# Modulation steps moved from the second layer's merge into the first layer's second feed-forward network, and another order of the first attention

## The chip, the core and the metric

One core of a Trainium2 chip runs the whole kernel. TensorE (PE in the rows) does the matrix products, VectorE (DVE) and ScalarE (ACT) the elementwise work, GpSimd (POOL) what is left over, and SyncE (SP) issues most loads. The metric is the device time in microseconds. The kernel before took 2209.5 us, the median of three runs from 2206.29 to 2209.86. The profiled execution took 2209.73 us; the span of its trace is 2207.9 us, so 1.8 us lie outside the trace.

## What is computed

Two layers of a trunk over 256 latent tokens and 256 context tokens, model width 1024, all in float32:

```
per layer:
  x += 1/2 * ffn_a(modulated norm(x))            # SwiGLU, width 2816
  u  = modulated norm(x) @ w_in                  # split into q, kv, differential q/k/v, pool, three gates
  x += gate * (sigmoid(g0)*A(u) + sigmoid(g1)*B(u) + sigmoid(g2)*C(u)) @ w_out
  x += 1/2 * ffn_b(modulated norm(x))            # SwiGLU, width 2816
output: final RMS norm of the latent tokens
```

A is latent attention with 8 heads, B differential attention with 8 heads (two softmax maps each), C a pooling over 2, 4, 8 and 16 neighbours. The modulation of a layer is nine vectors of 1024 values (shift, scale and gate for each of the three parts), each the product of a 1024 x 1024 matrix with the conditioning vector of the latent tokens, and with that of the context tokens. In the second layer only the latent tokens go on after the attention's keys are made, so its vectors m = 5 to 8 are needed for one stream only.

## The kernel before, in words

**Weights.** A float32 product is made of three products of split operands (`mm3`, line 292): hi times hi, lo times hi, hi times lo. Every weight comes as a chunk of 128 x 1024 (512 KB). `Weights.split` (line 131) loads it into a raw buffer (line 142, queue of SP), ScalarE casts the upper part `hi` (line 143), and VectorE or GpSimd subtracts it to get `lo` (line 147). GpSimd makes `lo` where `on_pool` is set; in both merges (after their first column) and in all that follows the second attention VectorE does. Four raw buffers (`RAW`) and four pairs hi/lo (`RING`) go round; a chunk is prepared up to three chunks ahead of its product.

**Modulation.** `ada_step` (line 249) is one of 144 steps of eighteen vectors: it loads 128 columns of one modulation matrix, 512 KB, into one of the same four raw buffers (line 259, SP), and VectorE multiplies and sums it with the conditioning vector (line 262, tile `junk`, one instruction per stream). The steps run in one fixed sequence; who calls `ada_step` takes the next one. Callers are the first feed-forward loop at its start, `FFN.step` (line 584) once per hidden block f, `FFN.middle` (line 612) once per output block, and the merge, once for each of its 24 branches (line 1369). When all 144 are done, a call does nothing.

**Stages.** Each layer is: first feed-forward network ("ffa"), attention and pooling ("mixing"), merge, second feed-forward network ("ffb"). A feed-forward network has 22 hidden blocks f of 128; 0 and 1 belong to the boundary, `FFN.middle` runs f = 2 to 13, then the first half of the output product, then f = 14 to 21. In the second layer's ffb each hidden block is half as long on TensorE, since 256 instead of 512 columns go through.

**Order of the attention.** `mixing` (line 1178) issues its instructions in an order written by hand, `SCHEDULE` (line 43): one string per layer, rounds between bars. For each attention unit a round runs the letters; before the round the unit's scores `a1` (tile `sc`) and its softmax `soft` (exponentials `pe` on ScalarE) are issued. `T` transposes the oldest waiting unit's probabilities on TensorE (tile `tr`; ScalarE casts `pth`, VectorE subtracts `ptl`), `V` multiplies them with the values (tile `po`), `N` runs the next piece of a normalisation, `P` and `D` switch `lo` between GpSimd and VectorE, and the other words are projections and their work: `q6` makes a query, `p1` a pooling group (scratch tiles `pp` and `pw`, mostly on GpSimd), `g12` a gate computed early, `k2`, `dk2` keys, and so on. Each engine executes its queue strictly in the order of issue, so the place of a word is its place in all queues.

Of the kernel before, what the change touches and what calls it, by code (L numbers as in the profile page):

```python
# [17 lines left out]
D = 1024  # L18
KD = 8
T = 512  # L20
# [20 lines left out]
WARM = 3  # L41
EARLY = ((68, 108), (271, 307))
SCHEDULE = (
# [138 lines left out]
class Kernel:  # L182
# [372 lines left out]
    class FFN:  # L555
# [28 lines left out]
        def step(self, f):  # L584
            K = self.K
            for up in (False, True):
                it = Kernel.FItem(self, f, up)
                if self.both:
                    it.mm(None)
                else:  # L590
                    it.part(range(KD))
                it.finish()
                self.early(up)
            K.ada_step()

        def early(self, store):
            if self.i == 0:
# [580 lines left out]
    def mixing(self):  # L1178
        nc = self.nc
        l = self.ml  # L1180
        both = len(self.qs) == 2
# [51 lines left out]
        kr, kr_copy = self.kr_item()  # L1233
# [37 lines left out]
        def fetch(dm):  # L1271
            for b in (2, 1, 0):
                if (dm, b) in early:
                    fetched[dm, b] = t = self.pg("sg")
                    nc.sync.dma_start(t[:, c], early.pop((dm, b))[:, c])
# [6 lines left out]
        def settle():  # L1282
            self.run_later()
            done.update(soon)
            soon.clear()

        def step(text):


            for x in text.split():  # L1290
                if x == "N":
                    if cur:
                        cur.pop(0)()
                elif x in "PD":
                    self.on_pool = x == "P"
                elif x == "V":
                    n, pv = pvs.pop(0)
                    if pv:
                        assert need[n][1] in done, (n, need[n])
                        pv()  # L1300
                    if n in last:
                        done.add(last[n])
                elif x == "T":
                    n, u = trs.pop(0)
                    u.tr()
                    pvs.append((n, u.pv))
                else:
                    f, req = fill.pop(x)
                    assert all(y in done for y in req), (x, req)
                    before, self.later = self.later, []  # L1310
                    was = list(soon)
                    soon.clear()
                    f()
                    for y in before:
                        y()
                    done.update(was)
                    soon.append(x)
                    if not self.later:
                        settle()
        rounds = SCHEDULE[l].split("|")  # L1320
        step(rounds.pop(0))
        settle()
        for n, mk in enumerate(units):
            assert all(x in done for x in need[n][0]), (n, need[n])
            u = mk()
            u.a1()
            u.soft()
            if n in heads:
                done.add(f"u{heads[n]}")
            cur.extend(x for x in (u.norm, u.comb) if x)  # L1330
            step(rounds.pop(0))
            while cur:
                cur.pop(0)()
            settle()
            trs.append((n, u))
# [4 lines left out]
        for dm in range(KD):  # L1340
            ms = []
            if dm == 1:
                self.on_pool = False
            for b in (2, 1, 0):
                bias = self.v(V_BG + l * 24 + b * 8 + dm)
                if b == 2:
                    for n in ((0, 1) if dm == 0 else (dm + 1,)):
                        fetch(n)
                g = fetched.pop((dm, b), None)
                if g:  # L1350
                    nc.scalar.activation(g[:, c], g[:, c], AF.Sigmoid, bias=bias)
                else:
                    p = self.ps("gt")
                    self.gemm(p[:, c], self.win(l, C_GATE + b * D + dm * 128), self.u, c)
                    g = self.pg("sg")
                    nc.scalar.activation(g[:, c], p[:, c], AF.Sigmoid, bias=bias)
                if dm == 0:
                    step(rounds.pop(0))
                    settle()
                branch = (self.oml, self.odn, self.opool)[b]  # L1360
                pb_ = self.ps("br")
                self.gemm(pb_[:, c], [(names[b], l, i * 128, ((dm * 128, 128),)) for i in range(4)],
                          [branch[i] for i in range(4)], c)
                if dm == 0:
                    step(rounds.pop(0))
                    settle()
                nc.vector.tensor_tensor(out=g[:, c], in0=g[:, c], in1=pb_[:, c], op=ALU.mult)
                ms.append(g)
                self.ada_step()
                if dm == KD - 1 and b == 2:  # L1370
                    for j in range(KD):
                        self.back("X", self.X, j)
                if dm == KD - 1 and b != 0:
                    for i in ((0, 1, 2) if b == 2 else (3, 4, 5, 6)):
                        h, o = self.pg(f"mh{i}", F32R), self.pg(f"ml{i}", F32R)
                        self.split(merged[i][:, c], h[:, c], o[:, c])
                        merged[i] = (h, o)
            nc.gpsimd.tensor_tensor(out=ms[0][:, c], in0=ms[0][:, c], in1=ms[1][:, c], op=ALU.add)
            nc.vector.tensor_tensor(out=ms[0][:, c], in0=ms[0][:, c], in1=ms[2][:, c], op=ALU.add)
            merged.append(ms[0])  # L1380
# [337 lines left out]
```

## Time and profile before

| stage (window of the trace, us) | length | PE busy | DVE busy | POOL busy |
|---|---|---|---|---|
| start, ffa of layer 1 (0 to 437) | 437 | 404.17 | 285.20 | 177.79 |
| first attention (437 to 770) | 333 | 320.90 | 200.34 | 138.15 |
| first merge, ffb of layer 1 (770 to 1315) | 545 | 537.93 | 326.52 | 243.52 |
| ffa of layer 2 (1315 to 1623) | 308 | 308.00 | 184.27 | 113.76 |
| second attention (1623 to 1886) | 263 | 249.50 | 168.98 | 125.84 |
| second merge (1886 to 1980) | 94 | 84.91 | 70.65 | 16.25 |
| its output product (1980 to 2010) | 30 | 29.54 | 27.85 | 7.79 |
| ffb of layer 2 (2010 to 2133) | 123 | 123.00 | 79.26 | 0.18 |
| end (2133 to 2208) | 75 | 66.86 | 44.89 | 4.43 |
| span | 2207.9 | 2124.8 | 1388.0 | 827.7 |
| **profiled execution's own time** | **2209.73** | | | |

TensorE is busy for 96% of the span. What can be saved without taking products away is the time that it stands, and the time that it runs at half its clock. The mean granted clock of the run is 0.982 of full speed.

### The profile page before, as it was taken

To read this page: it belongs to the slowest core of one execution; us is meant where nothing else is said; L and a number is where in the kernel's file an instruction comes from. 1 tells how busy PE (TensorE), PEld (TensorE's weight loads), DVE (VectorE), ACT (ScalarE), POOL (GpSimd) and SP (SyncE) were. 2 spreads that over 40 slices of the span, in tenths; PEclk is the share of its full clock that TensorE was granted. 3 is DMA by queue.
4 is the path that set the end of the run, shared out by engine and by line. 5 is a ranking of instruction groups with operands and counts; after the bars stand their busy time and mean duration, and the time that the engine had idled before them with its cause. 6 is when DMAs were issued, how large, how long until landed. Compare 5 with 4: busy or idle time off the path is not lost.

```text
span 2207.9 us, 31032 instructions
## 1 busy us (share of the span) xinstructions
PE 2124.8 (96%) x11878; PEld 1826.3 (83%) x11878; DVE 1388.0 (63%) x2022; ACT 905.7 (41%) x1536; POOL 827.7 (37%) x582
## 2 busy tenths in 40 slices
PE   6799999999999999999999999999999999989998
PEld 3588888978787788888888898888888788889998
DVE  8866656455755699545545446665535776877755
ACT  3433233344565533332212243332334557446444
POOL 5434333322454521545544544333352347301000
PEclk8999999999999999999999999999999999999999
DMA  5468767174231277334444425776755452785553
GB/s 209 172 237 296 259 245 295 68 246 160 96 105 49 93 237 256 106 113 145 143 153 143 144 77 215 288 278 238 280 216 189 155 181 98 243 281 181 191 181 116
DMA packets 118806, 407.32 MB, mean 184 GB/s; under 512 B 13185, under 2 KB 16897, under 8 KB 118658
## 3 DMA queue, kind: packets, MB, share of 16 engines
q1 hardware_dynamic: 103106, 353.95, 46.7%
q10 hardware_dynamic: 15552, 51.39, 6.0%
q8 instruction: 93, 1.52, 0.3%
q14 instruction: 55, 0.45, 0.1%
HBM read 348.14 MB, written 57.15 MB: 184 GB/s over the span
## 4 chain that ended last, share of the span: by engine, by line
PE 79%; DVE 9%; ACT 5%; issue 3%; DMA 3%; POOL 2%; SPq 0%; ACTq 0%; DVEq 0%; POOLq 0%
PE dn L292 21%; PE fu L292 18%; PE fg L292 18%; PE gt L292 6%; PE it L292 6%; PE br L292 3%; PE vi L292 2%; DVE ul L410 1%; DVE junk L1463 1%; DMA w<-in_stream 1%; ACT pe L796 1%; ACT hi L143 1%; PE tr L843 1%; PE sc L1108 1%; DVE ptl L332 1%
## 5 line engine op out<-in xcount | busy, mean ns | idle before, releaser
L147 POOL TENSOR_TENSOR lo<-w,hi 128x1024 fp32r<-128x1024 f32 (+1 forms) x214 | 553.4, 2590 | 673.9 <-ACT hi L143 650.8
L143 ACT CAST hi<-w 128x1024 fp32r<-128x1024 f32 x359 | 374.9, 1048 | 614.0 <-DMA w<-in_stream 265.2
L262 DVE CUSTOM_DVE_ANT_0 junk<-a,cvec 128x1024 bf16<-128x1024 f32 x224 | 386.1, 1724 | 5.0 <-DMA a<-in_ada 1.7
L292 PE MATMUL dn<-hh,hi 128*128 128x512 f32 (+1 forms) x800 | 272.7, 341 | 0.0
L292 PE MATMUL dn<-hl,hi 128*128 128x512 f32 (+1 forms) x800 | 272.2, 340 | 0.0
L292 PE MATMUL dn<-hh,lo 128*128 128x512 f32 (+1 forms) x800 | 272.2, 340 | 0.0
L292 PE MATMUL fg<-ul,hi 128*128 128x512 f32 (+2 forms) x704 | 249.3, 354 | 1.6 <-DVE ul L410 1.6
L292 PE MATMUL fu<-uh,hi 128*128 128x512 f32 (+2 forms) x704 | 250.5, 356 | 0.0
L292 PE MATMUL fu<-ul,hi 128*128 128x512 f32 (+2 forms) x704 | 250.0, 355 | 0.0
L292 PE MATMUL fu<-uh,lo 128*128 128x512 f32 (+2 forms) x704 | 249.9, 355 | 0.0
L292 PE MATMUL fg<-uh,hi 128*128 128x512 f32 (+2 forms) x704 | 248.6, 353 | 0.0
L292 PE MATMUL fg<-uh,lo 128*128 128x512 f32 (+2 forms) x704 | 248.5, 353 | 0.0
L147 DVE TENSOR_TENSOR lo<-w,hi 128x1024 fp32r<-128x1024 f32 x147 | 179.9, 1229 | 106.4 <-ACT hi L143 106.0
L571 DVE TENSOR_TENSOR h<-sg,fu 128x512 f32<-128x512 f32 x66 | 45.3, 686 | 212.8 <-PE fu L292 130.1
L292 PEld LDWEIGHTS dn<-hl,hi 128*128 128x128 f32 x800 | 151.7, 190 | 17.0
L292 PEld LDWEIGHTS dn<-hh,lo 128*128 128x128 f32 x800 | 151.7, 190 | 16.9
L292 PEld LDWEIGHTS dn<-hh,hi 128*128 128x128 f32 x800 | 151.7, 190 | 16.8
L609 DVE SCALAR_TENSOR_TENSOR X<-dn,md,X 128x256 f32<-128x256 f32 x112 | 50.2, 480 | 161.0 <-PE dn L292 160.9
L292 PEld LDWEIGHTS fg<-ul,hi 128*128 128x128 f32 x704 | 132.8, 189 | 20.9 <-DVE ul L410 2.8
L292 PEld LDWEIGHTS fu<-ul,hi 128*128 128x128 f32 x704 | 134.5, 191 | 18.1
L292 PEld LDWEIGHTS fu<-uh,lo 128*128 128x128 f32 x704 | 134.4, 191 | 18.1
L292 PEld LDWEIGHTS fu<-uh,hi 128*128 128x128 f32 x704 | 134.5, 191 | 18.0
(321 smaller groups left out, 4507.1 us busy)
## 6 DMA issues: line engine op xcount, KB each, us to landing
w<-in_stream SPq DMA_DIRECT2D x360, 512.0 KB, 4.3
a<-in_ada SPq DMA_DIRECT2D x144, 512.0 KB, 4.7
el<-in_stream SPq DMA_DIRECT2D x46, 512.0 KB, 4.1
early<-eh ACTq DMA_DIRECT2D x46, 512.0 KB, 2.7
early<-el ACTq DMA_DIRECT2D x46, 512.0 KB, 3.7
hi<-early SPq DMA_DIRECT2D x46, 512.0 KB, 4.3
lo<-early SPq DMA_DIRECT2D x46, 512.0 KB, 5.4
g<-sg SPq DMA_DIRECT2D x13, 256.0 KB, 2.2
```

The source lines that it names most:

```text
L143: copy(hi, raw)
L147: eng.tensor_tensor(out=lo[:, c], in0=raw[:, c], in1=hi[:, c].bitcast(F32), op=ALU.subtract)
L262: nc.vector.tensor_tensor_reduce(out=self.junk, in0=raw, in1=self.cvec[:, s, :], scale=1.0, scalar=0.0, op0=ALU.mult, op1=ALU.add, accum_o ...
L292: nc.tensor.matmul(out, a, b, start=first and n == 0, stop=last and n == 2)
L332: nc.vector.tensor_tensor(out=lo, in0=src, in1=hi.bitcast(F32), op=ALU.subtract)
L410: self.nc.vector.scalar_tensor_tensor(out=lo, in0=t, scalar=sh, in1=hi.bitcast(F32), op0=ALU.add, op1=ALU.subtract)
L571: nc.vector.tensor_tensor(out=h[:, c], in0=sg[:, c], in1=pu[:, c], op=ALU.mult)
L609: nc.vector.scalar_tensor_tensor(out=x, in0=p[:, SC[s]], scalar=K.mod(self.l, m, s, dm), in1=x, op0=ALU.mult, op1=ALU.add)
L796: nc.scalar.activation(e[:, c], banks[i][:, c], AF.Exp, bias=nm[:, o:o + 1], scale=1.0, accum_out=ls[:, o:o + 1])
L843: nc.tensor.transpose(t[:, i * 128:i * 128 + 128], P[:, i * 128:i * 128 + 128], self.ident)
L1108: nc.tensor.matmul(out[qt], a[0:96, q0:q0 + 128], b[0:96, kc], start=n == 0, stop=n == 2)
L1463: nc.vector.tensor_tensor_reduce(out=self.junk, in0=ada[k][m], in1=self.cvec[:, s, :], scale=1.0, scalar=0.0, op0=ALU.mult, op1=ALU.add, a ...
```

## The change

1. The order of the first attention, `SCHEDULE[0]`, is another one, again 27 rounds. `q6` stands before `p1` instead of behind it, the gate `g11` is computed early instead of `g12`, and the letters T, V and N stand elsewhere in most rounds.
2. In `FFN.step` the call of `ada_step` goes into the loop over the two halves of a hidden block. Behind the second half it is called always, as before; behind the first half only in the first layer's ffb, for f not divisible by four with rest 3. That stage takes 15 more steps (43 instead of 28).
3. The merge calls `ada_step` in the first layer only. The second layer's merge takes none (22 before).

The total stays 144, in the same sequence. Counting the calls: the second layer's ffa takes 28 steps before and now, and 7 steps are left over for the second layer's ffb, behind f = 2 to 8, one instruction on VectorE each (they are columns 1 to 7 of the last vector, m = 8).

```diff
 SCHEDULE = (
...
-    "N k1 V T sq p3 | P k2 N mc | D q4 T V md N q5 V T N N D N k3 st N N | g40 T N ds1 N N pp3 | V p1 q6 N N p2 "
...
+    "sq p3 N | | P T k2 N mc T q4 D V md T V q5 k3 | D N N q6 st N pp3 N g40 | T N V ds1 p1 N N N p2 N g32 | dn2 "
...
@@ FFN.step
                 it.finish()
                 self.early(up)
-            K.ada_step()
+                if up or self.i == 2 and self.both and f % 4 != 3:
+                    K.ada_step()
@@ mixing, merge
                 ms.append(g)
-                self.ada_step()
+                if both:
+                    self.ada_step()
```

What this does to the queues is shown at three places.

ScalarE, late in the first attention, before: the copies of the two halves of `q6` (`qf_6130`), those of the pooling group p2 (`pp_6177`, `pp_6194`), and the cast of the query `qh6`.

```order
L983 COPY pp_6099<-it_6052 128x256
L143 CAST hi105_6121<-w105_6123 128x1024
L1068 COPY qf_6130<-it_6114 96x256
L1069 COPY qf_6130<-it_6114 64x256
L143 CAST hi106_6167<-w106_6169 128x1024
L983 COPY pp_6177<-it_6145 128x256
L983 COPY pp_6194<-it_6145 128x256
L334 ACTIVATE qh6_6137<-qf_6130 96x512
```

ScalarE at the same place of the change; the same projection's tiles are now `qf_5876` and `qh6_5883`.

```order
L1069 COPY qf_5876<-it_5860 96x256
L1070 COPY qf_5876<-it_5860 64x256
L340 ACT_TABLE_LOAD
L340 ACTIVATE tbl_5891<-cst0_75 128x1
L904 ACTIVATE r2_5890<-st2_5885,cst0_75 8x512
L340 ACT_TABLE_LOAD
L340 ACTIVATE tbl_5894<-cst0_75 128x1
L334 ACTIVATE qh6_5883<-qf_5876 96x512
```

The cast of `qh6` stands behind a statistic and two table loads, and no longer behind copies of a pooling group; those of p1 and p2 come 12 to 16 rows later.

SP, end of the second merge, before: loads of modulation columns (`a`), of weight chunks (`w`), the eight back-loads of X, and the first chunk of the output product (`w332_17368`).

```order
L142 DMA w330_17262<-in_stream 128x1024
L259 DMA a1_8_6_17279<-in_ada 128x1024
L142 DMA w331_17299<-in_stream 128x1024
L259 DMA a1_8_7_17331<-in_ada 128x1024
L1023 DMA X0_17337<-X10_13983 128x256
L1023 DMA X1_17339<-X11_13985 128x256
```

SP at the same place of the change:

```order
L142 DMA w329_17213<-in_stream 128x1024
L142 DMA w330_17246<-in_stream 128x1024
L142 DMA w331_17280<-in_stream 128x1024
L1024 DMA X0_17312<-X10_14034 128x256
L1024 DMA X1_17314<-X11_14036 128x256
```

No modulation load stands between the weights of this merge any more; the back-loads of X still stand ahead of `w332`.

VectorE, one hidden block of the second layer's ffb, before: two `lo`, then the evacuation of a block (`sg`, `fb`, `h`, `hl2`), then the next two `lo`.

```order
L147 TENSOR_TENSOR lo348_18013<-w348_18014,hi348_18012 128x1024
L575 TENSOR_TENSOR sg_18042<-fg_17980,rB_17952 128x256
L576 COPY fb_18044<-fg_17980 128x1
L575 TENSOR_TENSOR h_18043<-fu_18011,rB_17952 128x256
L576 COPY fb_18044<-fu_18011 128x1
L578 SCALAR_TENSOR_TENSOR h_18043<-h_18043,fb_18044,sg_18042 128x256
L332 TENSOR_TENSOR hl2_18052<-h_18043,hh2_18051 128x256
L147 TENSOR_TENSOR lo349_18057<-w349_18058,hi349_18056 128x1024
```

VectorE at the same place of the change:

```order
L576 COPY fb_18019<-fu_17986 128x1
L578 SCALAR_TENSOR_TENSOR h_18018<-h_18018,fb_18019,sg_18017 128x256
L332 TENSOR_TENSOR hl2_18027<-h_18018,hh2_18026 128x256
L262 ISA junk_78,mr18_13304<-a1_8_1_18030,cvec_77 128x1024
L262 ISA mr18_13304 128x1
L147 TENSOR_TENSOR lo349_18035<-w349_18036,hi349_18034 128x1024
```

A modulation sum and the reading of its result stand between the evacuation and the next `lo`, and so for seven blocks.

## Rows read from the trace of the kernel before

**Rows 1.** Busy time by windows: us, then busy us (count), PEclk, DMA share, GB/s.
```profile
437.00:770.00 333.00, 320.90 (x1782) 260.41 (x1782) 200.34 (x350) 177.22 (x414) 138.15 (x194) 0.97 0.36 124
951.00:1254.00 303.00, 303.00 (x1373) 252.38 (x1373) 156.35 (x177) 81.68 (x100) 155.43 (x57) 1.00 0.44 145
1886.00:1980.00 94.00, 84.91 (x671) 82.29 (x669) 70.65 (x111) 37.68 (x55) 16.25 (x9) 0.98 0.81 273
2010.00:2089.00 79.00, 79.00 (x657) 79.00 (x656) 56.25 (x110) 41.40 (x60) 0.18 (x1) 1.00 0.56 179
```

**Rows 2.** What PE waited for, 437 to 770 us: total us, times, longest.
```profile
PE sc L1108 <- ACT qh L334: 2.4, 1, 2.4
PE po L867 <- DVE ptl L332: 2.1, 2, 1.7
PE tr L843 <- DVE ri L1137: 1.9, 1, 1.9
PE sc L1108 <- ACT pe L1130: 1.6, 1, 1.6
...
PE it L292 <- ACT pe L796: 0.8, 1, 0.8
PE po L866 <- DVE mv L332: 0.8, 1, 0.8
```

**Rows 3.** Busy time by windows: stretches at half the clock.
```profile
600.67:604.08 3.41, 3.41 (x26) 2.69 (x19) 2.31 (x4) 0.90 (x2) 3.24 (x4) 0.50 0.14 58
...
723.55:730.38 6.83, 6.83 (x18) 4.33 (x17) 5.15 (x9) 3.39 (x11) 5.78 (x15) 0.50 0.47 154
1979.66:1986.49 6.83, 6.06 (x24) 5.42 (x25) 6.36 (x10) 4.11 (x9) 0.78 (x1) 0.50 0.77 275
```

**Rows 4.** Timeline of ACT around the cast of q6: start, us, row [idle before].
```profile
720.64 0.37 ACT L983 COPY pp<-it 128x256 f32<-128x256 f32 x1 [7.76 <-POOL pw L991]
720.91 0.63 ACT L334 ACTIVATE qh<-qf 96x512 fp32r<-96x512 f32 x1
```

**Rows 5.** Timeline of PE and DVE: two T and the ptl made from them.
```profile
496.78 1.11 PE L843 MATMUL tr<-cst,pe 128*128 128x128 f32 x8
...
504.70 1.29 DVE L332 TENSOR_TENSOR ptl<-tr,pth 128x512 fp32r<-128x512 f32 x2 [1.53 <-ACT pth L331]
...
542.74 1.03 PE L843 MATMUL tr<-cst,pe 128*128 128x128 f32 x8
...
546.49 1.28 DVE L332 TENSOR_TENSOR ptl<-tr,pth 128x512 fp32r<-128x512 f32 x2
```

**Rows 6.** What PE waited for, 1886 to 1990 us.
```profile
PE dn L292 <- ACT hi L143: 3.2, 1, 3.2
PE gt L292 <- DVE lo L147: 2.9, 3, 1.4
...
PE br L292 <- DVE lo L147: 0.8, 1, 0.8
```

**Rows 7.** Timeline of SP's queue, end of the second merge.
```profile
1968.04 0.33 SPq L259 DMA_DIRECT2D a<-in_ada  x1
1968.42 6.03 SPq L1023 DMA_DIRECT2D X<-X  x8
```

**Rows 8.** Timeline of DVE and PE in the second layer's ffb.
```profile
2030.25 2.36 DVE L147 TENSOR_TENSOR lo<-w,hi 128x1024 fp32r<-128x1024 f32 x2 [0.45 <-ACT hi L143]
...
2033.70 0.28 PE L292 MATMUL fu<-uh,lo 128*128 128x258 f32 x1
...
2035.50 2.36 DVE L147 TENSOR_TENSOR lo<-w,hi 128x1024 fp32r<-128x1024 f32 x2 [0.53 <-ACT hi L143]
```

**Rows 9.** Line 262 in the first layer's ffb (951 to 1254): ns min/median/max.
```profile
L262 DVE CUSTOM_DVE_ANT_0 junk<-a,cvec x54: 1214/1226/3297, 972.9 to 1246.1; 128x1024 bf16<-128x1024 f32 x54
L262 DVE DVE_READ_ACCUMULATOR2_ANT mr<- x54: 76/82/86, 974.0 to 1249.3; 128x1 f32 x54
```

**Rows 10.** The page's part 6, DMA issues: count, KB each, us to landing (median).
```profile
w<-in_stream SPq DMA_DIRECT2D x360, 512.0 KB, 4.3
```

10 rows, old and new, of the table SCHEDULE are left out of this document.

## The prediction

> **What bounds the kernel now.** TensorE does, nearly everywhere, so I read first the busy times by windows, stage by stage. In the first layer's ffb TensorE is busy for 303.00 of 303.00 us, in the second layer's for 79.00 of 79.00; in the first attention it stands for 333.00 - 320.90 = 12.1 us and in the second merge for 94.00 - 84.91 = 9.1 us [rows 1]. The change touches these four stages. Then I read TensorE's waits in the two that stand: in the attention they are single waits of 0.8 to 2.4 us, each on another engine's tile [rows 2], in the merge they are late weights [rows 6]. Last I read the granted clock. After several of these waits TensorE runs at 0.50 of its clock, that is at 1.2 instead of 2.4 GHz, for 3.41 or 6.83 us [rows 3]; the first attention has the two stretches shown and two more like the first, and the second merge's end has one. In such a stretch about half of TensorE's busy time is lost, so it is a second price of the same wait: 3 x 3.41/2 + 6.83/2 = 8.5 us in the attention, 6.06/2 = 3.0 us behind the merge. The waits near 1 us have no such stretch behind them, those of 1.6 us and more have.
>
> **The change part by part.**
>
> *The second merge.* 22 modulation steps leave it: 22 loads of 512 KB, 22 sums on VectorE. The DMA share is 0.81, at 273 GB/s, against 0.56 in the stage behind it [rows 1]; the loads share four raw buffers with the weights, and TensorE waits for the weights made from these: 2.9 and 0.8 us on `lo`, 3.2 us on the first `hi` of the output product [rows 6], 6.9 us in all (what else is under 0.6 us each, I leave out). The last is the plainest: SP issues the last modulation load at 1968.04, then needs 6.03 us for eight back-loads of X (one of them waits for that load's semaphore), and only then comes the chunk that TensorE waits for [rows 7]. In the change nothing stands between the weights, and the wait that holds that chunk back, for the raw buffer of the fourth chunk before, ends when VectorE has made that `lo`, some three chunks ahead of TensorE. X's eight issues stay ahead of it but cost 0.33 us each in the rows where nothing holds them, under 3 us against three chunks of 3.5 us (84.91 us for 24 chunks). I therefore expect all 6.9 us and the 3.0 us of the clock to go, less 0.4 us for what is late next (VectorE's evacuations): **-9.5 us**, bounds -6 (only the waits of the output product and its clock) and -10.5.
>
> *The second layer's ffb.* Seven steps come in, behind f = 2 to 8. VectorE makes each pair of `lo` 5.25 us after the pair before (2030.25 to 2035.50), while TensorE needs 48 products x 79.00/657 = 5.8 us for a block, so VectorE gains 0.55 us a block; the first `lo` of a pair is ready about 2.2 us ahead of its use (2030.25 + 1.2 against 2033.70) [rows 8]. A sum costs 1.22 us and its reading 0.08 [rows 9]; it fills the 0.45 to 0.53 us in which VectorE waits for `hi` there [rows 8]. So a block takes 5.25 + 1.30 - 0.5 = 6.05 us on VectorE: the lead falls by 0.8 us at the first step, to 1.4, and by 0.25 at each further one, to -0.1 after seven. That costs TensorE **+0.3 us** with the chain between the engines; bounds 0 and +3, the upper one if the raw buffers count too (three loads a block instead of two).
>
> *The first layer's ffb.* 15 steps more, 30 sums of 1.23 us [rows 9], which makes 37 + 2.5 us of VectorE's 303 - 156 = 147 free microseconds; DMA goes from 145 to some 171 GB/s, less than the 273 of the merge [rows 1]. TensorE never waits there. **0**, bounds 0 and +2. The cover is the lead of the weights, three chunks of 5.4 us each; without it a late weight would cost its whole delay. The second layer's ffa keeps its 28 loads and has fewer sums, 0.
>
> *The first attention, what goes.* `q6` no longer stands behind the pooling groups: on ScalarE its cast stood behind a copy that waited 7.76 us for GpSimd [rows 4], and TensorE waited 2.4 us for it [rows 2]; now TensorE has two projections, a gate and more between the copies and the scores. With its clock: 2.4 + 3.4. The wait for `ptl` (1.7 of the 2.1) goes, as this V now has a gate more in front of it: 1.7 + 1.7. The two waits for `ri` and `mv`, 1.9 + 0.8, stood where three T and V came in one round, now spread: with the clock 4.4. The wait of scores for the bank that ScalarE's exponentials held, 1.6 + 1.7, falls as T no longer stands right ahead of them. Of the 0.8 us for `pe` I take half. Sum: 5.8 + 3.4 + 4.4 + 3.3 + 0.4 = 17.3 us.
>
> *What comes.* What matters is how far V stands from its own T. Of T to the second half of `ptl` the rows show 547.77 - 543.77 = 4.0 us and 505.99 - 497.89 = 8.1 us, the longer one where ScalarE was busy with exponentials [rows 5]. A 512-column product takes 303/1373 = 0.22 us [rows 1]. In the new order "T dq2 T N V" leaves 6.3 us between T and V (11.8 before): 0 to 1.8, I take 1.0. A later "T V" has only the next scores between, 1.8 us (3.8 at the unit's place before): 2.4 us by the short latency, 6.3 by the long; I take 2.4, as the row with the short one is the same kind of unit, and it brings one stretch at half clock, 1.7. The V behind `q0` and `k0` has 15 products, 3.4 us: +0.8. Near the end "N T | V V" is 0.7 us shorter than before: +0.7. Sum 6.6 us, bounds 2 and 16. Together **-10.7 us**, bounds -15 and -1.
>
> *Sum.* -9.5 + 0.3 + 0 - 10.7 = -19.9 us. From the profiled execution's 2209.73 us that is 2189.8, told as 2190; this execution lies 0.2 us above the median of 2209.5, so nothing is to be shifted. A measurement of this kernel tells about 0.2%, 4.4 us, from no change.
>
> **The rivals.**
>
> *The order gives nothing back.* Ten V stand elsewhere than before, and a wait removed in one place may only make TensorE early for the next: the queue of GpSimd and ScalarE holds the same work. For it: five kinds of waits in the rows have five different causes [rows 2]. Against it: the largest, at `q6`, is plain queueing and its work is not moved closer to anything else. Then 2209.7 - 9.5 + 0.3 = 2200.5.
>
> *V too close to T (slower than before).* Seven of sixteen V stand within 6.5 us of their T: at 6.3, 1.8, 6.4, 3.4, 6.3, 6.5 and 1.5 us. If each `ptl` took the long 8.1 us [rows 5], they would wait 1.8 + 6.3 + 1.7 + 4.7 + 1.8 + 1.6 + 6.6 = 24.5 us and, each being over 1.5 us, lose 7 x 1.7 = 12 us by the clock: the attention at 36.5 - 17.3 = +19, the whole at 2219 us. It decides from about 7.5 us of latency, where waits and clock eat the 26.8 us gained. Against it: the long row has a reason, exponentials queued ahead of the casts, which holds for few of the seven.
>
> *VectorE bounds the second ffb.* If a load there takes 6 us rather than the median of 4.3 [rows 10], four raw buffers turn round in 6 + 1 + 1.2 = 8.2 us, three loads a block in 6.2 us, and seven blocks lose 2.8 us besides a stretch at half clock: +4.5, the whole at 2194.
>
> *The first ffb pays for its loads.* VectorE's sum, which reads two operands from SBUF, takes 1.23 us at the median but up to 3.30 in this stage, where GpSimd works at the same time (155.43 us of it) [rows 1, 9]. As a mechanism of this kernel: 30 more such sums hold up GpSimd's `lo`, a raw buffer's trip grows from some 8 us (load 4.3 [rows 10], cast about 1, split 155.43/57 = 2.7 [rows 1]) to over 12 us, and with four loads in most blocks of 10.9 us the weights fall behind. That is 1.5 us a block in 15 blocks, less the lead of some 16 us: +7, the whole at 2197. The Trainium skill says so much of the cause ("GPSIMD Engine Reference", "Key points"): GpSimd shares its SBUF interfaces with VectorE and contends with its instructions that have two SBUF inputs. By that rule every sum moved out of the merge, where GpSimd hardly works, into this stage becomes dearer; the longest row agrees, the median of 1.23 us says that most of them escape it.
>
> *Only gains.* The new V all find their `ptl` ready: 2209.7 - 17.3 - 10.5 = 2182.
>
> That the change does not do what it says is no case: in the order of its instructions the loads are gone from the merge.
>
> **How the numbers follow.** The forecast, 2184 to 2196 with its centre at 2190, gets 0.57; the order without gain 0.20; V too close 0.07; the second ffb 0.07; the first ffb 0.03; only gains 0.06. The range takes in all but the slow end: 2180 (the clock of one more stretch gone beyond "only gains") to 2204 (the order at its upper bound of -1, the merge at -6 and the ffb at +1). Faster by over 0.2%, that is below 2205: the forecast, most of "no gain" (0.14), both ffb cases (0.09) and "only gains", together 0.86. Within 0.2%: 0.08, where the merge also gives less, or V is close in some units only. Slower: 0.06, the rest of "V too close" and a little of "no gain".
>
> **What would show it.** In the second merge: no wait of TensorE for `hi` or `lo`, a DMA share near 0.55, no stretch at 0.50 behind it. In the second ffb: a sum on line 262 in each of seven blocks, leads of `lo` shrinking to about zero and growing again from f = 9. In the first ffb: 303 us of TensorE without a wait, and 43 loads of line 259. In the attention: no wait of `sc` for `qh`, waits of `po` for `ptl` of about 1 and 2.4 us near the second and the fourth V, two stretches at half clock at most. The prediction is wrong if the attention's sum of waits and lost clock is not near 10 us, or if the merge still waits for weights with nothing but weights in its queue.

## The result

The changed kernel takes 2182.59 us, the median of four runs from 2182.06 to 2188.72, against 2207.89 us for the kernel before (2205.96 to 2209.86); the ratio is 0.9892, with a 95% interval of 0.9871 to 0.9913. That is 25.3 us less. The forecast was 2190, by a sum of -19.9 us, in a range of 2180 to 2204: the time lies inside the range, the gain was forecast a fifth too small.

The page of the changed kernel, its span and part 1 (busy us, share of the span, instructions by engine):

```profile
span 2180.5 us, 31034 instructions
PE 2114.3 (97%) x11878; PEld 1820.4 (83%) x11878; DVE 1409.8 (65%) x2024; ACT 905.8 (42%) x1535; POOL 816.8 (37%) x580
```

Busy time by windows of the changed kernel, columns as in [rows 1]: the first attention, the first layer's ffb, the second merge, the second layer's ffb, and the stretch that begins with the second merge's output product.

```profile
437.00:762.00 325.00, 320.94 (x1818) 260.54 (x1817) 206.43 (x361) 179.24 (x418) 137.08 (x193) 1.00 0.38 131
951.00:1240.00 289.00, 289.00 (x1277) 239.38 (x1276) 215.91 (x239) 75.21 (x92) 149.32 (x53) 1.00 0.51 171
1877.00:1960.00 83.00, 83.00 (x682) 83.00 (x682) 48.30 (x66) 41.15 (x58) 8.32 (x9) 0.98 0.58 192
1990.00:2069.00 79.00, 79.00 (x656) 79.00 (x656) 63.94 (x129) 41.30 (x59) 0.00 (x0) 1.00 0.66 218
1956.27:1963.10 6.83, 6.83 (x59) 6.83 (x58) 4.74 (x8) 3.11 (x6) 0.00 (x0) 1.00 0.50 158
```

TensorE is busy without a break in the windows of the two feed-forward networks, as before. The first attention is 4 us short of full instead of 12, and its granted clock is 1.00 where it was 0.97. The second merge has no gap at all, its DMA share is 0.58 where [rows 1] had 0.81, and the output product starts at full clock, where [rows 3] had half.

What TensorE waited for in the changed kernel, from the first attention to the end of the first merge (425 to 904 us), the answer to [rows 2]:

```profile
PE pst L372 <- DVE acc L362: 1.0, 1, 1.0
PE po L868 <- DVE ptl L332: 0.8, 2, 0.5
PE po L867 <- ACT pth L331: 0.8, 2, 0.6
PE sc L781 <- ACT pe L797: 0.6, 2, 0.3
PE it L292 <- DVE ptl L332: 0.5, 1, 0.5
PE tr L844 <- ACT pth L331: 0.3, 1, 0.3
```

The first line is the wait in front of the attention, which the kernel before has too. Behind it no wait is longer than 0.6 us. In the second merge and its output product (1876 to 1975 us), the answer to [rows 6] is a single line, a wait for the attention's last result, which the kernel before has too:

```profile
PE br L292 <- DVE odl L332: 1.4, 1, 1.4
```

To see where the time went I took one instruction that each stage has in front of it, the statistic of a norm (line 372), as a mark. In the timeline of the kernel before (start us, us, row [idle before]) the first, second, fourth and fifth of these marks read:

```profile
425.35 0.47 PE L372 MATMUL pst<-pick,acc 128*128 128x2 f32 x3 [1.02 <-DVE acc L362]
...
936.18 0.56 PE L372 MATMUL pst<-pick,acc 128*128 128x2 f32 x2 [2.71 <-DVE acc L362]
...
1673.71 0.35 PE L372 MATMUL pst<-pick,acc 128*128 128x2 f32 x2 [1.02 <-DVE acc L362]
...
2016.86 0.39 PE L372 MATMUL pst<-pick,acc 128*128 128x2 f32 x3
```

The same four in the changed kernel's timeline:

```profile
425.24 0.47 PE L372 MATMUL pst<-pick,acc 128*128 128x2 f32 x3 [1.02 <-DVE acc L362]
...
921.30 0.34 PE L372 MATMUL pst<-pick,acc 128*128 128x2 f32 x1 [2.71 <-DVE acc L362]
...
1659.81 0.35 PE L372 MATMUL pst<-pick,acc 128*128 128x2 f32 x2 [1.02 <-DVE acc L362]
...
1989.47 0.39 PE L372 MATMUL pst<-pick,acc 128*128 128x2 f32 x3
```

The distances from mark to mark in the traces of before and after:

| from mark to mark | before | after | difference |
|---|---|---|---|
| first attention, first merge, its output product | 510.8 | 496.1 | -14.8 |
| ffb of layer 1 | 370.2 | 370.5 | +0.3 |
| ffa of layer 2 | 367.4 | 368.0 | +0.6 |
| second attention, second merge, its output product | 343.1 | 329.7 | -13.5 |
| ffb of layer 2 | 181.5 | 181.5 | 0.0 |

With 0.1 us at the start the sum is -27.4 us, the difference of the two spans. So there are two gains in two places, as forecast, and next to nothing is paid in the feed-forward networks. Both are larger than forecast in this pair of traces; the experiments below say how much of that is the kernel, and how much the pair.

### The profile page after: what moved, and what is told of

Read it like the earlier page. It is cut to its first block, busy times and chain, and to the rows that moved or that the text cites. A ratio compares the mean times of both kernels' runs of the same rounds, so it can differ in the third digit from the quotient of the medians.

```text
span 2180.5 us, 31034 instructions
## 1 busy us (share of the span) xinstructions
PE 2114.3 (97%) x11878; PEld 1820.4 (83%) x11878; DVE 1409.8 (65%) x2024; ACT 905.8 (42%) x1535; POOL 816.8 (37%) x580
## 4 chain that ended last, share of the span: by engine, by line
PE 84%; DVE 7%; ACT 4%; issue 2%; POOL 1%; DMA 1%; SPq 0%; ACTq 0%; DVEq 0%; POOLq 0%
PE dn L292 21%; PE fu L292 19%; PE fg L292 18%; PE gt L292 8%; PE it L292 7%; PE br L292 4%; PE vi L292 2%; DVE ul L410 1%; DVE junk L1465 1%; ACT pe L797 1%; PE tr L844 1%; PE sc L1109 1%; DVE ut L400 1%; ACT hi L143 1%; PE po L868 0%
## 5 line engine op out<-in xcount | busy, mean ns | idle before, releaser
L262 DVE CUSTOM_DVE_ANT_0 junk<-a,cvec 128x1024 bf16<-128x1024 f32 x224 | 396.1, 1768 | 3.8
L292 PEld LDWEIGHTS fu<-uh,lo 128*128 128x128 f32 x704 | 134.7, 191 | 17.9
L292 PEld LDWEIGHTS fg<-uh,hi 128*128 128x128 f32 x704 | 133.1, 189 | 18.0
```

The costliest lines, as they stand in the source:

```text
L262: nc.vector.tensor_tensor_reduce(out=self.junk, in0=raw, in1=self.cvec[:, s, :], scale=1.0, scalar=0.0, op0=ALU.mult, op1=ALU.add, accum_o ...
L292: nc.tensor.matmul(out, a, b, start=first and n == 0, stop=last and n == 2)
```

## Experiments

**The two halves alone.** First the kernel before with only the new order:

```diff
-SCHEDULE = (<the order before>, ...)
+SCHEDULE = (<the order of the change>, ...)
```

> The kernel before with the new order of the first attention alone; modulation steps as before. Theory (the two halves of the change are separate, each in its own stage): the first attention gives what it gave in the whole change, 14.8 us between the same two marks, so about 2208 - 14.8 = 2193; the second merge still shows its waits for lo and hi (2.9, 0.8, 3.2 us) and the stretch at half clock behind it. Rival (the order's gain needs the lighter loads elsewhere, or moves into a later wait): less than 10 us, 2198 or more.

Measured: 2197.54 us against 2208.45, ratio 0.9944 (0.9927 to 0.9961), that is 10.9 us less (8.6 to 16.1). Its waits in the merge are much like those of before (3.2 and 0.8 us on `lo`, 2.0 us on the first `hi` of the output product). Then the moved steps, with the old order:

```diff
-            K.ada_step()
+                if up or self.i == 2 and self.both and f % 4 != 3:
+                    K.ada_step()
...
-                self.ada_step()
+                if both:
+                    self.ada_step()
```

> The kernel before with the modulation steps moved, order of the first attention as before. Theory: the second merge and what follows it give 13.0 us, the other stages nothing, so about 2208 - 13 + 1 (the two later feed-forward networks each took 0.3 to 0.6 us more in the whole change) = 2195 to 2196. By the prediction's term it would be 9.2 us, 2199. Rival (the first layer's second network pays for its loads): the marks around it lie 2 us or more further apart, 2197 or more.

Measured: 2194.04 us against 2208.45, ratio 0.9934 (0.9919 to 0.9949), that is 14.4 us less (11.3 to 17.9), with no wait in the merge. The halves add up: 10.9 + 14.4 = 25.3, the gain of the whole; with intervals this wide, that they meet it to the tenth is luck. The expectation of the first, 14.8 us, came from one pair of traces; it lies inside the interval, but the other traces speak for less. From the first mark to the statistic of the first merge, 16.7 us ahead of the second mark, they take 494.1, 491.2 and 491.4 us in the old order (before and two variants with the same attention), and 479.1 to 482.8 us, in the middle 479.9, in nine traces with the new one (in one of them with a T moved): 11.5 us between the middle values, close to the 10.7 forecast.

The steps read likewise. From the fourth mark to the fifth (second attention, merge, output product), three traces with the merge of before take 343.1, 345.9 and 338.9 us, and nine with the changed merge 326.8 to 329.7: 14.2 us between the middle values.

What makes traces of the same attention differ by some 3 us is mostly the clock. Of the nine with the new order, the seven whose stretch at half clock at the first mark is 3.41 us long take 479.1 to 481.3 us, the two where it is 6.83 us long 482.4 and 482.8. In the old order the trace of before has 20.5 us at half clock there, the two variants with the same attention 13.7 each. The same wait of 1.66 us for `ptl` stands in the kernel before, where a stretch at half clock follows [rows 3], and in the variant with the steps alone. There the products behind the same wait run at full clock, but another wait, 67 us later, has its stretch as before (a row of before, then rows of that variant, timeline of TensorE and busy time by windows):

```profile
599.12 0.45 PE L867 MATMUL po<-ptl,dv 128*64 128x256 f32 x2 [1.66 <-DVE ptl L332]
```

```profile
598.07 0.45 PE L868 MATMUL po<-ptl,dv 128*64 128x256 f32 x2 [1.66 <-DVE ptl L332]
...
599.73:603.14 3.41, 3.41 (x29) 2.77 (x22) 2.41 (x4) 0.80 (x2) 3.24 (x4) 1.00 0.17 70
667.40:670.81 3.41, 3.41 (x18) 3.41 (x17) 1.51 (x5) 3.41 (x13) 3.41 (x4) 0.51 0.00 0
```

So a wait of that size costs its stretch in some executions and not in others.

**The end of the merge alone.** Three steps go from the merge to the first layer's ffb, so that the last five of the 24 branches carry none:

```diff
                     K.ada_step()
+            if self.i == 2 and self.both and f in (2, 6, 10):
+                K.ada_step()
```

> The kernel before with only three steps moved, from the end of the second merge to the first layer's second network (behind f = 2, 6 and 10), so that the last five branches of the merge carry no modulation load. Theory: the 3.2 us of the output product's first chunk, 0.5 us behind it and the clock of the 6.83 us stretch go, 7.1 us by the shift of the products in the whole change, 2201; the waits for lo inside the merge stay (about 5 of 5.9 us). Rival (the loads of the whole merge are behind, and the last chunk is only where it shows): the wait moves into an earlier branch, 2204 or more.

Measured: 2201.33 us against 2208.45, ratio 0.9965 (0.9952 to 0.9978), -7.1 us. TensorE's waits there (1886 to 1990 us):

```profile
PE br L292 <- DVE odl L332: 1.4, 1, 1.4
PE gt L292 <- DVE lo L147: 1.1, 2, 0.6
PE br L292 <- ACT odh L331: 0.6, 1, 0.6
PE dn L292 <- DVE ml L332: 0.5, 2, 0.3
PE br L292 <- DVE lo L147: 0.3, 1, 0.3
```

The wait for `hi` of the output product's first chunk is gone, as the theory has it. X's back-loads still stand ahead of that chunk, so it was the modulation loads that made it late. Matched product by product with the changed kernel's trace, the stretch behind the merge loses 7.1, 7.0 and 6.4 us in three traces with the merge of before, and 1.1 here: this one chunk is worth about 6 us. The expectation was off for the inside of the merge, where about 5 of 5.9 us were to stay: this trace loses 2.9 us there. But the three traces with the merge of before lose 5.9, 2.8 and 7.9, so whether the waits inside became smaller can't be told from one trace.

**q6 alone.** The kernel before with two words exchanged:

```diff
-V p1 q6 N N p2
+V q6 p1 N N p2
```

> The kernel before with one swap in the first attention: q6 ahead of p1 instead of behind it. Theory: the wait of the scores for the cast of q6 (2.4 us) and the 6.83 us at half clock behind it go, 5.8 us, 2202, if the copies of p1 and p2 hold nothing else up. Rival (ScalarE's queue only swaps what is late: the exponentials and casts behind the copies of p1 and p2 now come late): a new wait of 2 us or more at the next transposes or values, 2206 to 2209.

Measured: 2207.06 us against 2208.45, ratio 0.9995 (0.9983 to 1.0007): no change that can be told. The ten runs spread from 2200.88 to 2211.65, and the profiled one is the fastest, so its rows show where the waits are, and not the median. The wait for `qh` is gone, and in its place stand (timeline of TensorE, the rows with a wait):

```profile
721.18 0.63 PE L843 MATMUL tr<-cst,pe 128*128 128x128 f32 x4 [0.20 <-ACT sg L1263]
723.20 0.63 PE L843 MATMUL tr<-cst,pe 128*128 128x128 f32 x4 [1.40 <-POOL pp L982]
724.64 0.50 PE L292 MATMUL it<-uh,hi 128*128 128x512 f32 x1 [0.81 <-ACT pe L1130]
```

That is 0.2 + 1.4 + 0.8 = 2.4 us for the 2.4 that went, and again a stretch at half clock, 3.41 us long (6.83 before). The rival was right in its time, and its one new wait of 2 us or more is spread over three: a copy of p2 still holds ScalarE up for 7.07 us, and the gate's copy (`sg`) and the exponentials (`pe`) now stand behind it. That the new order gains here because it also takes a gate, projections and other units' transposes in between is argued from its rows; no run shows it alone.

**A V close to its T.** The changed kernel, with the T of one unit moved from 29 us ahead of its V to right in front of it:

```diff
-g40 | T N V ds1 p1 N N N p2 N g32 | dn2 g60 om0 ds2 q7 V N g11 T
+g40 | N V ds1 p1 N N N p2 N g32 | dn2 g60 om0 ds2 q7 T V N g11 T
```

> The changed kernel with one T of the first attention moved: the unit whose T stood 29 us ahead of its V now has it right in front of V. Theory of the slower rival's price: V waits for the casts and ptl of three parts, 4.0 to 5.3 us, and a stretch at half clock of 3.41 or 6.83 us follows: +6 to +9 us, about 2189 to 2191. Rival (ScalarE's queue is free there and TensorE waits only as long as the cast of the first part): 2 to 3 us and no stretch at half clock, about 2185.

Measured: 2184.14 us, 1.6 above the changed kernel's 2182.59, with before at 2207.96 in this comparison. The V in question (timeline of TensorE):

```profile
709.34 1.36 PE L835 MATMUL tr<-cst,pe 128*128 128x128 f32 x11
711.08 0.38 PE L858 MATMUL po<-pth,mv 128*128 128x256 f32 x1 [0.38 <-ACT pth L322]
712.45 0.45 PE L859 MATMUL po<-ptl,mv 128*64 128x256 f32 x2 [0.99 <-DVE ptl L323]
```

From the end of T to the end of the second `ptl` it is 1.7 us, 712.40 - 710.70, no stretch at half clock follows, and the third part of `ptl` is made while V runs. Here ScalarE has no exponentials ahead of the casts; in both rows of [rows 5], with 4.0 and 8.1 us, it has. So for this unit the slower rival's price does not hold.

**The same trick in the second attention.** In the changed kernel the scores of q3 wait 3.7 us for its cast. Exchanging q3 and q4 in the second layer's order:

```diff
-k0 q1 q4 P T N V p3 k1 N ma | mb q3 T V q5 k2
+k0 q1 q3 P T N V p3 k1 N ma | mb q4 T V q5 k2
```

> The changed kernel with one swap in the second attention's order: q3 where q4 stood and q4 where q3 stood, one round later. In the changed kernel the scores of q3 wait 3.7 us for its cast (ScalarE waits for GpSimd's part of the rotation, which stands behind a lo) and a stretch at half clock follows. Theory (the same kind of wait as at q6): both go, -3.7 - 1.7 = -5.4 us, about 2177. Rival (q4's scores come late instead, or the work ahead moves the wait to the values): -2 us or less.

Measured: 2185.11 us, ratio to before 0.9895 where the changed kernel has 0.9892 and 0.9894 (its second measurement, below): no gain. TensorE's waits there (1780 to 1830 us):

```profile
PE tr L835 <- POOL pe L1131: 3.8, 1, 3.8
PE st L943 <- ACT sq L934: 2.0, 1, 2.0
PE sc L1100 <- ACT pth L322: 0.5, 1, 0.5
```

The scores are in time, and the transposes behind them wait 3.8 us instead, for probabilities that GpSimd scales late. As with q6, one word moves a wait of this chain and does not remove it. This trace shows one thing more, in a stage that the swap does not touch: in the second layer's ffb (1990 to 2069 us) TensorE waits twice, and the stage takes 183.0 us where the first trace of the changed kernel has 181.5.

```profile
PE fu L283 <- DVE lo L138: 0.8, 2, 0.4
```

**What the second ffb has left.** The changed kernel with more work behind f = 2 to 8: a second load and sum, a sum without a load, a load without a sum (read by an instruction of one column). The results of the extra work are not used.

```diff
                     K.ada_step()
+            if self.i == 2 and not self.both and f <= 8:
+                K.ada_extra(f)     # load 512 KB and sum it; or one of the two
```

> The changed kernel with a second modulation load and sum behind each of f = 2 to 8 of the second layer's ffb, into a tile that nothing reads. Theory (VectorE sets the pace there: in the changed kernel its pairs of lo come every 5.78 us, one step having added 0.53 us, against 5.8 us of TensorE a block): a second step has no idle time left to fill and adds 1.14 us, 6.92 a block, 1.1 us too long; seven blocks take 7.9 us, less the lead of 1.6 us: +6 us besides one to three stretches at half clock (1.7 each), +6 to +11, about 2190 to 2194. Rival (the lead is TensorE's own and VectorE has room): within 2 us of the changed kernel, 2182 to 2185.

> The changed kernel with a second sum behind each of f = 2 to 8 of the second layer's ffb, but without a load (it multiplies two vectors that are there). Theory A (VectorE's time sets the pace of that stage): 1.14 us more a block, 1.1 us too long, seven blocks less a lead of 1.6 us: +6 us over the changed kernel. Theory B (the four raw buffers set it: a chunk's load waits until the buffer's last reader is done): the sum alone delays those readers by 1.14 us but takes no buffer, +1 to +3.

> The changed kernel with a second modulation load behind each of f = 2 to 8 of the second layer's ffb, read by one short instruction (one column) instead of a sum. Theory A (VectorE): +0 to +1. Theory B (raw buffers): four loads a block through four buffers, a trip of some 4.5 us for the load, 1.05 for the cast and 1.2 for lo, 6.8 us a block instead of 5.8: seven blocks less the lead, +5.

> The changed kernel once more, on the same chip as the three runs beside it, since the granted clock differs a little from run to run: 2182 to 2186.

Measured: 2194.75 us for both (12.2 above the changed kernel's 2182.59, the kernel before being at 2207.96 and 2207.89 in the two comparisons; 6 to 11 were expected), and beside a new median of the changed kernel of 2185.47, 2192.63 for the sum alone (+7.2) and 2191.93 for the load alone (+6.5). The stage itself, from its mark to the last one, takes 181.5 us in the changed kernel, 189.2 with the sum, 190.8 with the load, 193.3 with both. TensorE's waits there, of the sum alone and then of the load alone (1990 to 2060 us):

```profile
PE fu L297 <- DVE lo L147: 6.1, 6, 1.3
```

```profile
PE fu L297 <- DVE lo L147: 4.8, 6, 1.2
PE fu L297 <- ACT hi L143: 2.1, 2, 1.4
```

Either is enough to make TensorE wait in six of the seven blocks. What VectorE itself waits for in that window tells the two apart, again the sum first:

```profile
DVE lo L147 <- ACT hi L143: 3.3, 4, 1.7
```

```profile
DVE lo L147 <- ACT hi L143: 11.7, 11, 2.8
```

With the sum VectorE seldom waits for `hi`, so its own time is too long; with the load the weights come late to it, and it never waits for the load that its short instruction reads. So with one step a block both VectorE's time and the weights' way through the raw buffers are near their limit: each theory holds for its own addition, and neither is the only bound. Whether the late weights come from the four buffers or from the transfers' own pace was not separated; the DMA rate there, 246 GB/s, is below the 273 of the merge before.

**Two steps in every block of the first ffb.**

```diff
-                if up or self.i == 2 and self.both and f % 4 != 3:
+                if up or self.i == 2 and self.both:
```

> The changed kernel with two modulation steps behind every f of the first layer's ffb (48 steps there instead of 43), so that two instead of seven are left for the second layer's ffb. Theory (both stages have room): no difference beyond 2 us, and the smallest lead of lo in the second ffb no longer falls below 1.6 us. Rival (the first ffb pays for its loads): four loads in every block of 10.9 us there, its two marks 2 us or more further apart.

Measured: 2186.02 us beside 2185.47, no difference that can be told. TensorE and VectorE in the first layer's ffb of this kernel (951 to 1240 us):

```profile
951.00:1240.00 289.00, 289.00 (x1277) 239.30 (x1276) 235.40 (x256) 75.92 (x93) 150.76 (x55) 1.00 0.55 179
```

VectorE is busy for 235 of 289 us and TensorE still never waits. With only two steps left, the leads of `lo` in the second ffb go from 1.2 us at the least up to 5.0 at the end of the first half, where in the changed kernel's two traces they fall to 0.89 and 0.06. The expectation said 1.6 at the least; the point that they grow again after the last step holds.

## Why the prediction was right, and which term was too small

*The first attention: right in its total, with errors that met.* Forecast -10.7 us, measured -10.9 with the order alone. The waits named as removed are gone. Of the new waits, that of the V with only scores in between was put at 2.4 us and a stretch at half clock. The rows show it spread over smaller ones: T ends at 533.91, the next scores wait 0.28 and 0.29 us for banks, the next transposes 0.34, and by V at 537.58 `ptl` is ready (timeline of TensorE in the changed kernel):

```profile
532.88 1.03 PE L844 MATMUL tr<-cst,pe 128*128 128x128 f32 x8
534.50 0.38 PE L781 MATMUL sc<-dk2h,dq2h 32*128 32x256 f32 x1 [0.28 <-ACT pe L797]
535.17 0.38 PE L781 MATMUL sc<-dk2h,dq2h 32*128 32x256 f32 x1 [0.29 <-ACT pe L797]
...
537.08 0.63 PE L844 MATMUL tr<-cst,pe 128*128 128x128 f32 x4 [0.34 <-ACT pth L331]
537.58 0.38 PE L867 MATMUL po<-pth,dv 128*128 128x256 f32 x1
```

The pair of traces of before and after can be added up. The waits that went had 9.6 us (8.8 forecast) and the new ones have 2.7 (4.9 forecast, without the clock), together -6.9. The clock gives -8.5, where the forecast had -8.5 + 1.7. A wait for an early `lo`, a line of the answer to [rows 2], is missing in this trace of the changed kernel and back in its second one, with 1.3 us; it is no gain of the order:

```profile
PE it L292 <- DMA lo<-early: 1.1, 1, 1.1
```

And at full clock TensorE's busy time is 1.8 us longer in the new order, which no term had and whose cause stays open. Together that makes the pair's -14.8. Against the other two traces of the old order the clock gives only 5.1, and the sum is near the measured -10.9. So the new waits were forecast too dear and the lost clock too certain, and that the total came out to 0.2 us is luck.

One reading of the clock was wrong: waits near 1 us can have a stretch at half clock behind them. At the first mark 1.02 us of waiting stand, and the granted clock is 0.50 from 426.59 us on in the trace of before and from 426.14 in the changed kernel's. On q6, the first reason (it stands ahead of the pooling groups) is not enough, as the swap alone shows; the second (more work in between) was not tried alone.

*The second merge: right in its mechanism, too small.* Forecast -9.5 us; the steps alone give -14.4 in time, outside the bounds of -6 and -10.5, and the merge's own products, matched one by one in the traces of before and after, 13.0. Inside the merge the products of before fall behind by 5.9 us in this trace, where the sum had taken 3.7 from the rows of waits [rows 6]; as told above, two other traces with this merge lose 2.8 and 7.9 there. Behind it 7.1 us are lost in the first 24 products of the output product, where the sum had 3.2 + 3.0 [rows 3, 6]; a wait of 0.5 us was left out of it. And the 0.4 us for what would be late next never came. Most of what was missing inside is in how an idle time is read. One of the merge's waits, in the trace of before (timeline of TensorE):

```profile
1938.59 0.28 PE L292 MATMUL gt<-uh,hi 128*128 128x256 f32 x1
1938.71 0.28 PE L292 MATMUL gt<-ul,hi 128*128 128x256 f32 x1
1940.41 0.39 PE L292 MATMUL gt<-uh,lo 128*128 128x256 f32 x1 [1.41 <-DVE lo L147]
1940.63 0.28 PE L292 MATMUL gt<-uh,hi 128*128 128x256 f32 x1
1940.75 0.28 PE L292 MATMUL gt<-ul,hi 128*128 128x256 f32 x1
```

Products follow each other every 0.12 us, though each row is 0.28 us long. Without the wait the third would start at 1938.83, so it is 1.58 us late, not 1.41, and the one behind it loses another 0.10. The wait costs 1.68 us. The merge of before has five waits with an idle time in the rows, and two places more where the products slip by 0.28 us without one. Seven times 0.27 us, and a wait of 0.3 us that the prediction had left out, make the 2.2 us that were missing.

*The second ffb: right.* Forecast +0.3, with the lead of `lo` falling to -0.1 after seven steps; measured 0.0 in the pair of traces. In the changed kernel's two traces the least lead is 0.89 and 0.06 us, and TensorE has no idle time in the rows there; the trace with q3 and q4 exchanged, which has the same instructions in this stage, has 0.8 us of it. So the stage stands at its limit. The lead does not fall step by step, as the sum had it. A step adds 0.53 us to VectorE's period (5.25 to 5.78), where the sum had 0.8, since consecutive instructions overlap by about 0.08 us each; that is still within TensorE's 5.8 a block, and the lead stays as it is. What takes it away are single late `hi`: in the second trace VectorE waits 1.13 us for one, and the lead falls from 1.6 to 0.4 there. The seven sums are there, one a block, none of them slowed:

```profile
L262 DVE CUSTOM_DVE_ANT_0 junk<-a,cvec x7: 1217/1218/1220, 2002.3 to 2037.4; 128x1024 bf16<-128x1024 f32 x7
```

*The first ffb: right, nothing.* 84 sums in its window instead of 54, the longest now 3.46 us:

```profile
L262 DVE CUSTOM_DVE_ANT_0 junk<-a,cvec x84: 1211/1226/3458, 948.3 to 1238.4; 128x1024 bf16<-128x1024 f32 x84
```

The median is where it was [rows 9], and it hides the dearer ones: 39 of the 84 sums take over 2 us, where 24 of the 54 did before, and those of the usual 3.3 us run beside an instruction of GpSimd for 2.2 us. VectorE's busy time in the window grew by 60 us (156.35 to 215.91), where the sum had 37 + 2.5. What the Trainium skill says of GpSimd and VectorE sharing their SBUF interfaces ("GPSIMD Engine Reference", "Key points") fits these long sums. They moved no time: TensorE has over 6 us of lead in this window in every chunk.

*The rivals.* "V too close" lost: the new waits for `ptl` are 0.5 us at most. "The order gives nothing back" is refuted by the order alone, though it describes the single swaps well. "VectorE bounds the second ffb" did not happen in the pair, and is near: one more sum or one more load a block brings it. "Only gains" named 2182, and the time measured first, 2182.59, is nearer to that than to the forecast's 2190, and outside the 2184 to 2196 that the forecast had as its own (the second, 2185.47, is inside). But its mechanism is not what happened: `ptl` is still waited for, and the time came from the merge, which gave more than any of its bounds.

Open is which of the order's many moved words carry its 10.9 us; only q6 was tried alone.

## What to carry to other kernels

Prefetch work for a later stage belongs in the stage whose engines and buffers have room, and a stage that is nearly full has to be counted per step: the step's load, its buffer and its engine time each have to fit into the block. A wait seen in an order written by hand belongs to a chain of queues; in both tries here, to exchange two words only moved it. When waits are summed up, add to each idle time what the rows do not show, here 0.27 us, and count a lost clock as likely, not as certain. Take more than one trace before a gain of a few microseconds is put down to a stage: here single traces of the same instructions differ by 3 us and more.

## What was not expected of the hardware

An idle time of TensorE in the rows is shorter than what the wait costs: by 0.16 us, since a product's row lasts 0.28 us where the next one starts after 0.12, and by 0.10 us for the first product after it. The same wait of 1.66 us was followed by 3.41 us at half clock (granted 0.50) in one execution and by full clock (1.00) in another. In the first layer's ffb 39 of VectorE's 84 sums took over 2 us instead of 1.22, most of them 3.3 beside an instruction of GpSimd, and the median did not show it.
